# Splitting weights early and moving the decisions of a bitwise top-k search to GpSimd, in a two-layer encoder on one Trainium2 core

## The chip, the cores and the metric

The kernel runs on one core of one Trainium2 chip. The engines are named as in the profile: PE (TensorE matmul), PEld (its weight loads), DVE (VectorE), ACT (ScalarE), POOL (GpSimd) and SP (SyncE, which here only issues transfers). The metric is the device time of one execution in microseconds. PE's clock has two levels, 1.2 and 2.4 GHz; the profile gives the granted share of full speed.

## The reference

A trunk of two layers over 1040 tokens (16 meta tokens and 1024 frames) of width 1024. Layer 0 mixes tokens by chunked gated linear attention (GLA), layer 1 by sparse attention (DSA), and each is followed by a SwiGLU FFN. Of the DSA layer, this matters here:

```
proj = h @ w_in                              # split: q, c, q_idx, k_idx, w_idx
c = rmsnorm(c, g_kv)                         # latent, 256 wide
s_idx = einsum('bqhd,bsd->bqhs', qib, k_idx) * IDX_DIM ** -0.5
score = einsum('bqhs,bqh->bqs', relu(s_idx), wb)
score = where(key_chunk <= q_chunk, score, -inf)
top_val, top_idx = lax.top_k(score, 256)     # 256 keys per query
...
logits = q . (c[top_idx] @ w_uk) + bias[top_idx]
p = softmax(where(valid, logits, -inf)); o = (p @ c_sel) @ w_uv; return o @ w_out
swiglu(h) = (silu(h @ w_gate) * (h @ w_up)) @ w_out
```

All of it is float32. The selection by `top_k` is exact: ties go to the lower index.

## The kernel before

**Precision.** A float32 product is made of three matmuls in a faster format (`fp32r`): each operand is split into a high half (a cast) and a low half (operand minus high), and `PE` adds high x high, low x high and high x low (lines 198 to 200). So each weight tile that is loaded has to be split: `load_split` loads pieces of up to 1056 columns into a raw slot on SP's queue, ACT casts the high half (L186; GpSimd in the search, L188), and DVE or GpSimd subtracts for the low one (L189). Activations are split by `split` (L193 on ACT, L194 on DVE or GpSimd). Split weights stand in a ring of slots (`wh`, `wl`); `Weights.get` hands out a weight and loads the next one.

**Stages.** GLA to about 430 us; first FFN to 1245; index keys, index queries and scores to about 1382; the top-k search to about 1566 and the masks to 1605; attention to about 1850; then the attention's output weights and the second FFN. In the FFN a hidden unit (`hidden`) multiplies 128 gate and 128 up columns for a chunk of about 344 tokens, has ACT take silu into a slot `sg` of three, and has DVE multiply.

**The top-k search** (`topk`). Scores stand in `sc`, one block of 128 queries x nkeys, with nkeys 272, 400, 528, 656, 784, 912 and 1040 for blocks 1 to 7. For each query the 256th largest score is found bit by bit: a candidate threshold is counted against the keys, and the count decides the bit. The seven blocks form two groups, A (blocks 7, 1, 4, 3) and B (5, 2, 6). ACT counts 7 and 1 of A and 5 of B (L1047, a sign with an accumulator), DVE the others (L1053, a compare with an accumulator). Bits 31 to 16 are searched on the upper 16 bits of each score read as a bfloat16 number; bits 31 and 23 are counted on DVE alone. After each count come tiny operations on one column per block, all on DVE: `below` (L1062), `cand` (L1070), `flip` (L1073) and a second `flip` (L1076) in the upper half. `turnover` then takes the lower 16 bits of the keys that equal the threshold, as ordered numbers (ACT, L1103), and bits 15 to 0 follow with L1114, L1115 and L1117. While one group's tiny operations wait, the other group is counted: `rounds` writes them interleaved. At the end the seven masks are made (L1166 to L1174), with a running sum over ties.

**What runs beside it.** While the search goes, the code also emits PE's work in units: nine latent tiles (`latent`: 256 columns, root mean square by `row_rstd`, six tiny operations and a square root for each tile, then two transposes), 24 query units (`queries`, one head and a third of the frames each, drained by ACT into `qf`, L1000), the splits of queries (`parts`, L194; heads 3 to 5 on GpSimd) and the keys of the first head pair. Each unit has a cost, and as the units' costs add up, one step of the search is emitted for each share. Engines work their queues in the order of emission.

Of the kernel before, what the change touches and what calls it, by code (L numbers as in the profile page):

```python
# [22 lines left out]
TOPK = 256  # L23
# [56 lines left out]
class Weights:  # L80
# [28 lines left out]
class Trunk:  # L109
    def __init__(self, ctx, tc, io, out):  # L110
# [9 lines left out]
        self.whigh = None  # L120
# [55 lines left out]
    def load_split(self, src, n, pool=None, tags=("wh", "wl"), cap=RING, raw=None, piece=RAW):  # L176
# [4 lines left out]
        for a in range(0, n, piece):  # L181
            e = min(n, a + piece)
            r = raw() if raw else self.rawp.tile([128, RAW], F32, name="wraw")
            nc.sync.dma_start(r[:, : e - a], src[:, a:e])
            if self.whigh is None:
                nc.scalar.copy(hi[:, a:e], r[:, : e - a])  # L186
            else:
                self.whigh.tensor_copy(hi[:, a:e], r[:, : e - a])  # L188
# [474 lines left out]
    def ffn(self, pool, tmp, chunks, last_chunks, squares, after):  # L663
# [4 lines left out]
        def hidden(hh, hl, wi, q, a, n):  # L668
# [4 lines left out]
            t = tmp.tile([128, 512], F32, name="t")  # L673
# [21 lines left out]
        for g in range(G):  # L695
# [53 lines left out]
            prev = (hh, hl)  # L749

    def ffn_phase(self, layer, begun, norm_row, last_chunks, after, emit=None, cover=()):
# [3 lines left out]
        with ExitStack() as ctx:  # L755
# [36 lines left out]
            self.ffn(pool, tmp, chunks, last_chunks, squares, ended)  # L792
# [7 lines left out]
    def index_begin(self):  # L800
# [7 lines left out]
        def first():  # L808
            self.wlow = self.nc.gpsimd
# [11 lines left out]
    def dsa(self):  # L821
# [3 lines left out]
        with ExitStack() as ctx:  # L825
            self.wlow = nc.gpsimd
# [78 lines left out]
            with tc.tile_pool(name="topk", bufs=1) as tp, tc.tile_pool(name="cn", bufs=2) as cp:  # L905
# [3 lines left out]
                self.whigh = nc.gpsimd  # L909

                def parts(c, j):
# [3 lines left out]
                    self.split(self.xh[:, hs, t], self.xl[:, hs, t], qf[:, hs, a - META : a - META + n],  # L915
# [38 lines left out]
    def latent(self, pool, qf, cth, ctl):  # L954
# [5 lines left out]
        def unit(i):  # L960
            if i == 0:
                st["w"] = w.get("c")
# [514 lines left out]
```

## Time and profile before

| | |
|---|---|
| median of 3 runs | 2663.42 us (2662.87 to 2664.26) |
| profiled execution | 2667.23 us, its span 2665.0 us |
| mean granted clock of PE | 0.975 |
| PE busy | 2530.1 us, 95% of the span |
| DVE busy | 1417.1 us, 53% |
| ACT busy | 965.7 us, 36% |
| POOL busy | 255.2 us, 10% |
| weights in the DSA layer's queue | kidx, qidx (2), c, dq (4), ukv (4), do (4) |

The busy shares are averages over stages with different limits: 53% of DVE over the span says nothing of the 220 us in which it works without a break. The profiled execution is 3.8 us longer than the median, and sums over its rows are to be made against 2667.2. Times of day in the rows (1508.29) count from the span's start. Operations on one engine overlap by some hundredths of a microsecond, so that durations add up to slightly more than the busy time.

### The profile page before, as it was taken

What the parts mean: (1) busy time and instruction counts of PE and PEld (TensorE: products, weight loads), DVE (VectorE), ACT (ScalarE), POOL (GpSimd) and SP (SyncE); (2) the same over time, 40 slices, a digit from 0 to 9 for tenths busy, and PEclk for the clock granted to TensorE, in tenths of its full rate; (3) what the DMA queues carried; (4) which work ended last, traced back from release to release, by engine and by line L of the source; (5) the groups of instructions that cost most, each with busy time, mean ns of one, the idle gap of its engine ahead of it and who ended that gap; (6) DMA issues with size and microseconds to landing.
All of it is one profiled execution on the core that took longest, in us unless ns stands there. A gap on an engine that the chain in (4) does not pass through costs nothing.

```text
span 2665.0 us, 37404 instructions
## 1 busy us (share of the span) xinstructions
PE 2530.1 (95%) x15072; PEld 2342.3 (88%) x15072; DVE 1417.1 (53%) x3196; ACT 965.7 (36%) x1981; POOL 255.2 (10%) x222
## 2 busy tenths in 40 slices
PE   7999999999999999999898749999999999999997
PEld 6899999999999999999778739999988888888887
DVE  7565565643333333345699997673633333333346
ACT  5654452521111111114475667772511111111114
POOL 3000000200000000001212125540200000000001
PEclk9899999999999999999998969999999999999999
DMA  3113113011111111112100001012011111111111
GB/s 116 40 35 105 39 38 108 32 53 43 48 48 48 48 48 48 48 56 91 39 17 33 25 1 41 25 45 107 32 48 48 48 48 48 48 48 48 48 48 64
DMA packets 45168, 133.32 MB, mean 50 GB/s; under 512 B 4442, under 2 KB 15986, under 8 KB 44995
## 3 DMA queue, kind: packets, MB, share of 16 engines
q1 hardware_dynamic: 43634, 125.99, 14.0%
q0 software_dynamic: 1360, 4.95, 0.7%
q8 instruction: 118, 1.93, 0.3%
q14 instruction: 56, 0.45, 0.1%
HBM read 122.43 MB, written 13.27 MB: 51 GB/s over the span
## 4 chain that ended last, share of the span: by engine, by line
PE 79%; DVE 12%; issue 4%; ACT 3%; POOL 1%; DMA 0%; SPq 0%; ACTq 0%; DVEq 0%; POOLq 0%
PE ps L198 25%; PE ps L200 25%; PE ps L199 25%; DVE jd L1053 4%; PE ps L1282 1%; DVE sc L877 1%; POOL xl L194 1%; PE ps L499 1%; DVE no L304 1%; DVE xl L194 0%; DVE flip L1073 0%; PE ps L218 0%; PE ps L1294 0%; ACT L292 0%; DVE na L267 0%
## 5 line engine op out<-in xcount | busy, mean ns | idle before, releaser
L198 PE MATMUL ps<-xh,wh 128*128 128x344 f32 (+6 forms) x2808 | 951.0, 339 | 21.8 <-ACT qf L1000 12.3
L200 PE MATMUL ps<-xh,wl 128*128 128x344 f32 (+6 forms) x2808 | 944.2, 336 | 3.5 <-DVE wl L189 3.1
L199 PE MATMUL ps<-xl,wh 128*128 128x344 f32 (+6 forms) x2808 | 946.1, 337 | 1.3 <-POOL xl L194 0.9
L198 PEld LDWEIGHTS ps<-xh,wh 128*128 128x128 f32 x2808 | 532.2, 190 | 55.9 <-ACT qf L1000 14.7
L199 PEld LDWEIGHTS ps<-xl,wh 128*128 128x128 f32 x2808 | 532.5, 190 | 31.2 <-POOL xl L194 1.8
L200 PEld LDWEIGHTS ps<-xh,wl 128*128 128x128 f32 x2808 | 532.5, 190 | 30.6 <-DVE wl L189 3.3
L675 DVE TENSOR_TENSOR t<-sg,ps 128x344 f32<-128x344 f32 (+4 forms) x116 | 65.1, 561 | 653.5 <-PE ps L200 652.6
L186 ACT CAST wh<-wraw 128x1056 fp32r<-128x1056 f32 (+2 forms) x175 | 179.4, 1049 | 593.4 <-PE ps L199 588.3
L688 DVE TENSOR_TENSOR h<-h,ps 128x344 f32<-128x344 f32 (+3 forms) x456 | 251.3, 567 | 168.0 <-PE ps L200 167.9
L198 PE MATMUL ps<-hh,wh 128*128 128x512 f32 (+2 forms) x800 | 280.3, 350 | 0.0
L199 PE MATMUL ps<-hl,wh 128*128 128x512 f32 (+2 forms) x800 | 280.0, 350 | 0.0
L200 PE MATMUL ps<-hh,wl 128*128 128x512 f32 (+2 forms) x800 | 279.8, 350 | 0.0
L189 DVE TENSOR_TENSOR wl<-wraw,wh 128x1056 fp32r<-128x1056 f32 (+2 forms) x167 | 201.8, 1230 | 78.0 <-ACT wh L186 77.0
L198 PE MATMUL ps<-wh,xh 128*128 128x256 f32 (+9 forms) x560 | 174.8, 312 | 16.1 <-ACT xh L193 6.9
L200 PE MATMUL ps<-wh,xl 128*128 128x256 f32 (+9 forms) x560 | 168.7, 301 | 3.6 <-POOL xl L194 1.6
L194 POOL TENSOR_TENSOR xl<-no,xh 128x344 fp32r<-128x344 f32 (+5 forms) x52 | 59.5, 1150 | 1164.6 <-ACT xh L193 1164.5
L674 ACT ACTIVATE sg<-ps 128x344 f32<-128x344 f32 (+4 forms) x116 | 57.8, 498 | 304.0 <-PE ps L200 303.9
L199 PE MATMUL ps<-wl,xh 128*128 128x256 f32 (+9 forms) x560 | 167.2, 299 | 0.0
L193 ACT CAST hh<-t 128x344 fp32r<-128x344 f32 (+4 forms) x116 | 60.0, 517 | 285.0 <-DVE t L675 285.0
L198 PEld LDWEIGHTS ps<-hh,wh 128*128 128x128 f32 x800 | 150.0, 188 | 14.6
L199 PEld LDWEIGHTS ps<-hl,wh 128*128 128x128 f32 x800 | 150.3, 188 | 14.3
L200 PEld LDWEIGHTS ps<-hh,wl 128*128 128x128 f32 x800 | 150.5, 188 | 13.9
(283 smaller groups left out, 3376.4 us busy)
## 6 DMA issues: line engine op xcount, KB each, us to landing
wraw<-in_w_fi SPq DMA_DIRECT2D x44, 528.0 KB, 3.7
wraw<-in_w_fi SPq DMA_DIRECT2D x44, 496.0 KB, 4.8
wraw<-in_w_fo SPq DMA_DIRECT2D x22, 528.0 KB, 3.8
wraw<-in_w_fo SPq DMA_DIRECT2D x22, 496.0 KB, 4.8
s_skew<-s_rel POOLq DMA_DIRECT2D x8, 583.5 KB, 12.5
h<-in_ht SPq DMA_DIRECT2D x8, 520.0 KB, 5.5
wraw<-s_skew SPq DMA_DIRECT2D x8, 520.0 KB, 3.4
h<-s_h SPq DMA_DIRECT2D x8, 512.0 KB, 6.1
```

Of the source, the lines that this page charges most:

```text
L186: nc.scalar.copy(hi[:, a:e], r[:, : e - a])
L189: self.wlow.tensor_sub(lo[:, a:e], r[:, : e - a], hi[:, a:e].bitcast(F32))
L193: self.nc.scalar.copy(hi, src)
L194: (low or self.nc.vector).tensor_sub(lo, src, hi.bitcast(F32))
L198: mm(p, sh, mh, start=first, stop=False, skip_group_check=True)
L199: mm(p, sh, ml, start=False, stop=False, skip_group_check=True)
L200: mm(p, sl, mh, start=False, stop=last, skip_group_check=True)
L304: v.scalar_tensor_tensor(o, x, self.gains[:, row, k : k + 1], y, op0=OP.mult, op1=OP.mult)
L674: nc.scalar.activation(sg[:, :n], pg[:, :n], AF.Silu)
L675: v.tensor_mul(t[:, :n], sg[:, :n], pu[:, :n])
L688: v.tensor_add(self.h[:, d, a : a + n], self.h[:, d, a : a + n], p[:, :n])
L1053: v.tensor_scalar(j[:, : nkeys(b)], src(b), cand, None, op0=op, op1=OP.add, accum_out=out)
```

## The change

Four things change.

**Weights split early** (`split_early`, `load_parts`). All weights of the DSA layer (kidx, qidx, c, dq, ukv, do: 54 pieces of 512 columns) are loaded in the first FFN, one piece after each call of `hidden`; GpSimd makes both halves (L213, L214), and SP stores them to HBM (L216). Where the DSA layer needs a weight, GpSimd's queue loads both halves (L200), and nothing is split there any more. `sg` slots hold the raw pieces, and `t` shrinks to 352 columns in layer 0.

**The upper half on ordered numbers** (`signs`). Instead of bit 31 on bfloat16 numbers, the sign is counted on DVE from the upper 16 bits as integers; then ACT rewrites each block's upper halves as ordered unsigned numbers, scaled by plus or minus one (L1147). The other 15 upper bits are searched as the lower 16 are, the same seven blocks on the same engines in each bit, with float candidates.

**Decisions on GpSimd** (`decide`). The tiny operations after a count are four on GpSimd: a subtraction (L1102), a compare and multiply (L1103), an addition that gives the candidate (L1104), and the next `flip` (L1106). They are kept in order by `issue_after`.

**Latent norms by three** (`row_rstd` on three columns): the tiny operations run once for three tiles. In the masks, compare and subtraction become one operation, and the queries' low halves on GpSimd are three instructions per chunk instead of one.

DVE's queue in the lower half of the search, two rounds before, word for word; names end in the number of the buffer: group A's count is cnt_13074, its candidate cand_13079, group B's cnt_13097 and cand_13102.

```order
L1053 TENSOR_SCALAR jd,cnt_13097<-mask,cand_13102 128x400
L1053 TENSOR_SCALAR jd,cnt_13097<-mask,cand_13102 128x912
L1114 TENSOR_TENSOR below_13078<-cnt_13074,thr_13077 128x4
L1115 SCALAR_TENSOR_TENSOR cand_13079<-below_13078,flip_13080 128x4
L1117 TENSOR_SCALAR flip_13080<-cand_13079 128x4
L1053 TENSOR_SCALAR jd,cnt_13074<-mask,cand_13079 128x656
L1053 TENSOR_SCALAR jd,cnt_13074<-mask,cand_13079 128x528
L1114 TENSOR_TENSOR below_13101<-cnt_13097,thr_13100 128x3
L1115 SCALAR_TENSOR_TENSOR cand_13102<-below_13101,flip_13103 128x3
```

The same queue after, in the upper half, from a round without other work (group A's candidate is cand_13479, group B's cand_13498):

```order
L1093 TENSOR_SCALAR jd,cnt_13475<-mask,cand_13479 128x656
L1093 TENSOR_SCALAR jd,cnt_13475<-mask,cand_13479 128x528
L1093 TENSOR_SCALAR jd,cnt_13494<-mask,cand_13498 128x400
L1093 TENSOR_SCALAR jd,cnt_13494<-mask,cand_13498 128x912
L1093 TENSOR_SCALAR jd,cnt_13475<-mask,cand_13479 128x656
```

What moved: nothing but counts is left between counts; the tiny operations are gone from this queue.

GpSimd's queue in the search before: splits of weights, the first head pair's bias, and the low halves of the queries.

```order
L188 CAST wh<-wraw 128x1056
L188 CAST wh<-wraw 128x992
L189 TENSOR_TENSOR wl<-wraw,wh 128x1056
L189 TENSOR_TENSOR wl<-wraw,wh 128x992
L188 CAST uh<-wraw 128x1024
L189 TENSOR_TENSOR ul<-wraw,uh 128x1024
L1235 TENSOR_TENSOR sc<-wraw,mask 128x144
L194 TENSOR_TENSOR xl<-qf,xh 128x3x344 x2
```

The same queue after, from the upper half, with the loads of one weight's halves (s_dq) and their waits:

```order
L1104 TENSOR_TENSOR cand_13498<-below_13497,flip_13499 128x3 [waits Pool_49]
L1106 TENSOR_SCALAR flip_13499<-cand_13498 128x3 [waits Pool_49]
L200 DMA wl<-s_dq_l 128x2048 [waits DMASW5_49,PE_49]
L1102 TENSOR_TENSOR below_13478<-cnt_13475,thr_13477 128x4 [waits DVE_49,Activation_49]
L200 DMA wh<-s_dq_h 128x2048 [waits DMASW4_49,PE_49]
L1103 TENSOR_SCALAR below_13478<-below_13478 128x4 [waits Pool_49]
L1104 TENSOR_TENSOR cand_13479<-below_13478,flip_13480 128x4 [waits Pool_49]
L1106 TENSOR_SCALAR flip_13480<-cand_13479 128x4 [waits Pool_49]
```

What moved: eight tiny operations a bit stand here, each with a wait for the one before it, and two loads stand between decisions and wait for PE.

SP's queue in the first FFN before:

```order
L184 DMA wraw<-in_w_fi 128x1056
L184 DMA wraw<-in_w_fi 128x992
L184 DMA wraw<-in_w_fi 128x1056
L184 DMA wraw<-in_w_fi 128x992
L184 DMA wraw<-in_w_fo 128x1056
L184 DMA wraw<-in_w_fo 128x992
```

And after, where each piece is a load and two stores:

```order
L190 DMA wraw<-in_w_fi 128x992 [waits DMAHW7_49,DVE_49]
L190 DMA wraw<-in_w_fo 128x1056 [waits DMAHW6_49,DVE_49]
L190 DMA wraw<-in_w_fo 128x992 [waits DMAHW7_49,DMAHW1_49,DVE_49]
L212 DMA sg<-in_w_qidx 128x512 [waits DMAHW3_49,DMAHW2_49]
L216 DMA s_qidx_h<-eh 128x512 [waits Pool_49]
L216 DMA s_qidx_l<-el 128x512 [waits DMAHW4_49,Pool_49]
L212 DMA sg<-in_w_qidx 128x512 [waits DMAHW5_49,DVE_49]
L216 DMA s_qidx_h<-eh 128x512 [waits Pool_49]
L216 DMA s_qidx_l<-el 128x512 [waits Pool_49]
```

What moved: three pieces stand between two FFN weights, and their stores wait for GpSimd.

The diff, cut to its core:

```diff
+            name, src, n = self.seq[i]
+            self.tiles[i] = self.k.load_parts(name, n) if src is None else self.k.load_split(src, n)
...
+    def load_parts(self, name, n, pool=None, tags=("wh", "wl"), cap=RING):
+
+        pool = pool or self.ring
+        ts = [pool.tile([128, cap], F32R, name=t) for t in tags]
+        for t, src in zip(ts, self.parts[name]):
+            self.nc.gpsimd.dma_start(t[:, :n], src)
+        return tuple(ts)
+
+    def split_early(self, pool, raw):
+
+        nc = self.nc
+        for name, src, n in self.early:
+            for a in range(0, n, PRE):
+                e = min(n, a + PRE)
+                r = raw()[:, : e - a]
+                hi = pool.tile([128, PRE], F32R, name="eh")[:, : e - a]
+                lo = pool.tile([128, PRE], F32R, name="el")[:, : e - a]
+                nc.sync.dma_start(r, src[:, a:e])
+                nc.gpsimd.tensor_copy(hi, r)
+                nc.gpsimd.tensor_sub(lo, r, hi.bitcast(F32))
+                for p, t in zip(self.parts[name], (hi, lo)):
+                    nc.sync.dma_start(p[:, a:e], t.bitcast(F32))
+                yield
...
-        s = pool.tile([128, 4], F32, name="rs")
-        x, y, t, r = (s[:, j : j + 1] for j in range(4))
+        m = ss.shape[1]
+        s = pool.tile([128, 4 * m], F32, name="rs")
+        x, y, t, r = (s[:, j * m : j * m + m] for j in range(4))
...
                     wi = w.get("fi%d" % (2 * g + q))
                     for a, n in chunks:
                         hidden(hh, hl, wi, q, a, n)
+                        next(beside, None)
...
-                    self.split(self.xh[:, hs, t], self.xl[:, hs, t], qf[:, hs, a - META : a - META + n],
-                               nc.gpsimd if j in QPOOL else v)
+                    if j in QPOOL:
+                        for hd in range(3 * j, 3 * j + 3):
+                            self.split(self.xh[:, hd, t], self.xl[:, hd, t], qf[:, hd, a - META : a - META + n],
+                                       nc.gpsimd)
+                        return
...
+            y = self.row_rstd(pool, st["ss"], 256)
+            for i, c, x, r in st["x"]:
+                v.scalar_tensor_tensor(c[:r, :], x[:r, :], y[:r, i % 3 : i % 3 + 1], self.gkv[:r, :],
+                                       op0=OP.mult, op1=OP.mult)
+                self.later.at(3 + i % 3, lambda i=i, c=c: turn(i, c))
...
-        def upper(g, bit):
-            below, cand, flip, pos = (g[k] for k in ("below", "cand", "flip", "pos"))
-            steps = [lambda: v.tensor_tensor(below, g["cnt"], g["all" if bit in (31, 23) else "thr"],
-                                             op=OP.is_gt)]
-            if bit == 31:
-                steps += [lambda: v.tensor_scalar(cand, below, 31, 0x3FFFFFFF,
-                                                  op0=OP.logical_shift_left, op1=OP.bitwise_xor),
-                          lambda: v.tensor_scalar(pos, below, 1, None, op0=OP.bitwise_xor)]
-            else:
-
-                steps += [lambda: v.scalar_tensor_tensor(cand, below, bit, flip,
-                                                         op0=OP.logical_shift_left, op1=OP.bitwise_xor)]
-            if bit > 16:
-                steps += [lambda: v.scalar_tensor_tensor(flip, pos, bit - 1, cand,
-                                                         op0=OP.logical_shift_left, op1=OP.bitwise_xor)]
-            if bit > 17:
-                steps += [lambda: v.tensor_scalar(flip, flip, 1 << (bit - 2), None, op0=OP.bitwise_xor)]
-            return steps
+        def decide(g, bit):
+
+            below, cand, flip = g["below"], g["cand"], g["flip"]
+
+            with ExitStack() as after:
+                if last:
+                    after.enter_context(self.tc.issue_after(last[0]))
+                gp.tensor_sub(below, g["cnt"], g["thr"])
+                gp.tensor_scalar(below, below, 0.0, -(2.0 ** bit), op0=OP.is_gt, op1=OP.mult)
+                last[:] = [gp.tensor_add(cand, below, flip).ins]
+                if bit:
+                    last[:] = [gp.tensor_scalar_add(flip, cand, 2.0 ** (bit - 2) if bit > 1 else 0.5).ins]
+
+        def start(g, bits):
+            v.memset(g["cand"], 2.0 ** (bits - 1) - 0.5)
+            v.memset(g["flip"], 2.0 ** (bits - 1) + 2.0 ** (bits - 2) - 0.5)
...
+        def rounds(bits):
+            for bit in range(bits - 1, -1, -1):
+                for g in groups:
+                    if bit < bits - 1:
+                        decide(g, bit + 1)
+                    count(g)
+                    yield
...
+        def signs(g):
+            for c, b in enumerate(g["b"]):
+                n = nkeys(b)
+                j = pool.tile([128, T], BF16, name="jd", tag="pre", bufs=2)
+                v.tensor_scalar(j[:, :n], half(b, 1), 2.0 ** 15, None, op0=OP.is_ge, op1=OP.add,
+                                accum_out=g["cnt"][:, c : c + 1])
+            sgn, add, x, y = (g[k] for k in ("sgn", "add", "x", "y"))
+            v.tensor_tensor(x, g["cnt"], g["all"], op=OP.is_gt)
+            v.tensor_scalar(sgn, x, -2.0, 1.0, op0=OP.mult, op1=OP.add)
+            v.tensor_scalar(add, x, 65535.0, None, op0=OP.mult)
+            v.scalar_tensor_tensor(y, x, -1.0, g["cnt"], op0=OP.add, op1=OP.mult)
+            more(g, y)
+            start(g, 15)
+            for c in list(range(g["na"], g["n"])) + list(range(g["na"])):
+                b = g["b"][c]
+                nc.scalar.activation(mu(b), half(b, 1), AF.Identity, bias=add[:, c : c + 1],
+                                     scale=sgn[:, c : c + 1])
...
-            v.tensor_scalar(eq, pre, need, None, op0=OP.is_le)
-            v.tensor_sub(sg, sg, eq)
-            v.tensor_scalar(mk(b), sg, 0.0, NEG, op0=OP.is_ge, op1=OP.mult)
+            v.scalar_tensor_tensor(sg, pre, need, sg, op0=OP.is_le, op1=OP.subtract)
+            v.tensor_scalar(mk(b), sg, 0.0, NEG, op0=OP.is_le, op1=OP.mult)
```

## Rows read from the trace of the kernel before

**Rows 1.** Windows by stage: us, busy us of each engine (count), PEclk, DMA share, GB/s.

```profile
600.00:650.00 50.00, 50.00 (x318) 50.00 (x318) 14.86 (x25) 9.00 (x15) 0.00 (x0) 1.00 0.16 55
1280.00:1360.00 80.00, 72.49 (x351) 62.43 (x349) 54.77 (x101) 45.85 (x102) 21.71 (x13) 0.91 0.12 42
1386.00:1478.50 92.50, 78.87 (x509) 77.59 (x508) 91.36 (x323) 46.11 (x119) 24.05 (x15) 0.93 0.12 39
1478.50:1500.50 22.00, 18.41 (x96) 17.66 (x96) 21.12 (x70) 12.88 (x24) 0.00 (x0) 0.84 0.02 8
1500.50:1566.40 65.90, 32.30 (x156) 29.29 (x156) 63.96 (x206) 47.64 (x102) 4.73 (x2) 0.75 0.00 1
1566.40:1605.00 38.60, 23.18 (x102) 18.72 (x103) 38.24 (x111) 20.39 (x53) 14.41 (x9) 0.68 0.00 0
```

**Rows 2.** What PE waited for, 1380 to 1610: us, times, longest.

```profile
PE ps L198 <- DVE xl L1009: 26.3, 3, 13.6
```

**Rows 3.** Timeline of DVE, one bit of the lower half: start us, us, operation.

```profile
1508.29 0.62 DVE L1053 TENSOR_SCALAR_CACHE_REDUCE jd<-mask,cand 128x400 bf16<-128x400 uint16 x1
...
1508.84 1.16 DVE L1053 TENSOR_SCALAR_CACHE_REDUCE jd<-mask,cand 128x912 bf16<-128x912 uint16 x1
...
1509.92 0.16 DVE L1114 TENSOR_TENSOR below<-cnt,thr 128x4 f32<-128x4 f32 x1
...
1510.39 0.89 DVE L1053 TENSOR_SCALAR_CACHE_REDUCE jd<-mask,cand 128x656 bf16<-128x656 uint16 x1
...
1511.89 0.15 DVE L1114 TENSOR_TENSOR below<-cnt,thr 128x3 f32<-128x3 f32 x1
...
1512.36 0.62 DVE L1053 TENSOR_SCALAR_CACHE_REDUCE jd<-mask,cand 128x400 bf16<-128x400 uint16 x1
```

**Rows 4.** Instruction groups of DVE, 1375 to 1605: count, busy us, mean ns, idle before.

```profile
L1073 DVE SCALAR_TENSOR_TENSOR flip<-pos,cand 128x4 int32<-128x4 int32 (+1 forms) x30 | 12.1, 403 | 0.5
...
L1062 DVE TENSOR_TENSOR below<-cnt,thr 128x4 int32<-128x4 f32 (+1 forms) x28 | 9.1, 327 | 0.0
L1070 DVE SCALAR_TENSOR_TENSOR cand<-below,flip 128x4 int32<-128x4 int32 (+1 forms) x30 | 8.4, 279 | 0.5
...
L1076 DVE TENSOR_SCALAR flip<-flip 128x4 int32<-128x4 int32 (+1 forms) x28 | 5.6, 199 | 0.0
```

**Rows 5.** Timeline of all engines, 1441 to 1449.

```profile
1443.78 4.77 POOL L189 TENSOR_TENSOR wl<-wraw,wh 128x1056 fp32r<-128x1056 f32 x2
...
1443.87 2.40 DVE L1073 SCALAR_TENSOR_TENSOR flip<-pos,cand 128x4 int32<-128x4 int32 x1
```

**Rows 6.** Instruction groups of ACT's counts, 1375 to 1605.

```profile
L1047 ACT ACTIVATE ja<-mask,cand 128x1040 bf16<-128x1040 uint16 (+5 forms) x90 | 78.5, 872 | 58.0 <-DVE cand L1070 31.3 <-DVE cand L1115 22.2 <-DVE cand L1065 2.9
L1047 ACT ACTIVATION_READ_ACCUMULATOR ja<-mask,cand 128x1 f32 x90 | 16.9, 188 | 0.0
```

**Rows 7.** Instruction groups of POOL by shape, whole span.

```profile
L194 POOL TENSOR_TENSOR xl<-no,xh 128x344 fp32r<-128x344 f32 x24 | 30.3, 1270 | 137.4 <-ACT xh L193 137.4
...
L332 POOL TENSOR_SCALAR w<-mean 96x128 fp32r<-96x128 f32 x4 | 2.0, 534 | 0.0
...
L194 POOL TENSOR_TENSOR xl<-no,xh 128x144 fp32r<-128x144 f32 x4 | 2.9, 727 | 4.1 <-ACT xh L193 4.1
...
L972 POOL MEMSET css<- 128x1 f32 x1 | 0.2, 186 | 0.0
```

**Rows 8.** Instruction groups of DVE's score sums by shape, 1300 to 1390.

```profile
L877 DVE SCALAR_TENSOR_TENSOR sc<-rt,wx,sc 128x328 f32<-128x328 f32 x14 | 6.7, 554 | 0.0
...
L877 DVE SCALAR_TENSOR_TENSOR sc<-rt,wx,sc 128x272 f32<-128x272 f32 x7 | 6.2, 891 | 0.2
```

**Rows 9.** The page: a PE group, a DMA queue, an FFN weight's load.

```profile
L200 PE MATMUL ps<-xh,wl 128*128 128x344 f32 (+6 forms) x2808 | 944.2, 336 | 3.5 <-DVE wl L189 3.1
...
q0 software_dynamic: 1360, 4.95, 0.7%
...
wraw<-in_w_fo SPq DMA_DIRECT2D x22, 528.0 KB, 3.8
```

More of the change, by code (lines that the diff above doesn't have):

```diff
@@ L958, in latent @@
         st = {}
+        slot = lambda j: qf.rearrange("p h t -> p (h t)")[:, j * 256 : j * 256 + 256]
         def unit(i):
@@ L1040, in count @@
-        def count(g, op, all_v=False, src=mk):
-            vs = []
-            for c, b in enumerate(g["b"]):
-                cand, out = g["cand"][:, c : c + 1].bitcast(F32), g["cnt"][:, c : c + 1]
-                if c < g["na"] and not all_v:
+        groups, last = [], []
+        for j, (blocks, na) in enumerate(GROUPS):
+            g = {"b": blocks, "n": len(blocks), "na": na}
+            for name, dt in (("cnt", F32), ("all", F32), ("thr", F32), ("below", F32), ("cand", F32),
+                             ("flip", F32), ("sgn", F32), ("add", F32), ("th", I32), ("x", F32), ("y", F32)):
+                g[name] = pool.tile([128, g["n"]], dt, name=f"{name}{j}")
+            for c, b in enumerate(blocks):
+                v.memset(g["all"][:, c : c + 1], nkeys(b) - float(TOPK))
+                v.memset(g["thr"][:, c : c + 1], nkeys(b) - (2.0 if c < na else 1.0) * TOPK)
+            groups.append(g)
@@ L1109, in turnover @@
-            v.memset(cand.bitcast(F32), 2.0 ** 15 - 0.5)
-            v.memset(g["flip"].bitcast(F32), 2.0 ** 15 + 2.0 ** 14 - 0.5)
-        def lower(g, bit):
-            below, cand, flip = (g[k].bitcast(F32) for k in ("below", "cand", "flip"))
-            return [lambda: v.tensor_tensor(below, g["cnt"], g["thr"], op=OP.is_gt),
-                    lambda: v.scalar_tensor_tensor(cand, below, -(2.0 ** bit), flip, op0=OP.mult,
-                                                   op1=OP.add),
-                    lambda: v.tensor_scalar(flip, cand, 2.0 ** (bit - 2) if bit > 1 else 0.5, None,
-                                            op0=OP.add)]
@@ L1120, in rounds @@
-        def rounds(bits, decide, op, src=mk):
-            counts, carry = [], []
-            for bit in bits:
-                for g in groups:
-                    tiny = decide(g, bit + 1) if bit < bits[0] else []
-                    for x in tiny[:1] + carry + counts[:1] + tiny[1:2]:
-                        x()
-                    rest = counts[1:]
-                    counts = count(g, op(bit), bit in (31, 23), src)
-                    for x in rest + tiny[2:3]:
-                        x()
-                    carry = tiny[3:]
-                    yield
-            for x in carry + counts:
-                x()
@@ L1138, in topk @@
-        for b in range(1, 8):
-            (v.tensor_copy if b % 2 else nc.scalar.copy)(mk(b).bitcast(U16), half(b, 1))
-        yield
-        yield from rounds(range(31, 15, -1), upper, lambda bit: OP.is_lt if bit == 31 else OP.is_le)
-        for g in groups:
-            for x in upper(g, 16):
-                x()
+                low = pool.tile([128, T], U16, name="low", tag="sg", bufs=2)[:, :n]
+                nc.scalar.activation(low, half(b, 0), AF.Identity, bias=g["add"][:, c : c + 1],
+                                     scale=g["sgn"][:, c : c + 1])
@@ L1145, in topk @@
+                v.scalar_tensor_tensor(mu(b), mu(b), tc, low, op0=OP.is_equal, op1=OP.mult)
+            more(g, g["cnt"])
+            bits_of(g, 1)
+            start(g, 16)
+        for g in groups:
+            signs(g)
+            yield
+        yield from rounds(15)
+        for g in groups:
+            decide(g, 0)
             turnover(g)
             yield
-        yield from rounds(range(15, -1, -1), lower, lambda bit: OP.is_lt, lambda b: mk(b).bitcast(U16))
+        yield from rounds(16)
```

159 lines of the change are left out of this document (70 added, 89 removed).

## The prediction

> **What bounds the kernel now.** I read the windows by stage first, then what TensorE waits for, then single instructions of one stage. In the windows [rows 1] the reader is to look at the two busy columns of PE and DVE. In a slice of the first FFN PE is busy 50.00 of 50 us and DVE 14.86: that stage is PE's, and everything else there is beside it. Between 1386 and 1605, the search for the 256 best keys and the masks, it is the other way round: DVE is busy 91.36 of 92.5, 21.12 of 22.0, 63.96 of 65.9 and 38.24 of 38.6 us, PE only 78.87, 18.41, 32.30 and 23.18. So PE stands still for 66 of these 219 us. Its largest wait is for DVE: 26.3 us in three waits for the low halves of the last queries [rows 2], which DVE reaches only in its turn between counts. A change is worth there what it takes off DVE, until the next engine binds.
>
> One bit of the lower half (one row for each group of blocks) is read from the timeline [rows 3]: group B's counts run 1508.29 to 1509.92 (1.63 us), three tiny operations to 1510.39 (0.47), group A's counts to 1511.89 (1.50), three tiny ones to 1512.36 (0.47): 4.07 us, of which 3.13 are counting. In the upper half the same bit takes far longer: the four tiny groups there sum to 9.1 + 12.1 + 8.4 + 5.6 = 35.2 us [rows 4], because some are stretched. One flip, of a kind that lasts 0.16 us undisturbed [rows 3], lasts 2.40 us while GpSimd subtracts weights from 1443.78 on for 4.77 us [rows 5].
>
> **The change, part by part.** The sum is made against the profiled execution, 2667.2 us (span 2665.0 and 2.2 around it), 3.8 us above the median of 2663.4; the 3.8 is taken off at the end.
>
> *The length of a bit afterwards.* Four things can set it, and the longest does. DVE: 3.13, counts alone. ACT: its counts and accumulator reads are (78.5 + 16.9) / 30 = 3.18 us a bit [rows 6], a little less where spans overlap; it drains queries too, so about 3.4. GpSimd: eight tiny operations, four a group. No row has a tiny operation on it. The nearest are a memset of one column, 186 ns, and a tensor_scalar of 128 columns, 534 ns; two subtractions of 144 and 344 columns, 727 and 1270 ns, lie on a line that starts at 0.34 and rises by 2.7 ns a column [rows 7]. I take 0.35, the line's start, since four columns add 0.01; eight make 2.8 (1.5 to 4.3 by the ends). The loop of group A: ACT's part of its counts, 1312 of 2096 columns of 3.18, is 2.0; then three operations until the candidate stands, 1.05; two hand-overs between engines, for which no row stands and I put 0.1 each, an estimate below the 0.16 that a tiny operation on DVE takes with all its passing on (three dependent ones in 0.47); together 3.25. I take 3.4. The bounds are 3.13, where only counting is left, and 4.3, where an operation costs 0.534.
>
> *Upper half* (92.5 us). Counting took 14 bits at 3.13 and bit 23 with all seven on DVE, and the rest of bit 31: 43.8 + 6.0 + 4.1 = 54 (the three blocks that ACT has elsewhere, 2.9 us, from the slope of [rows 3]: 400 columns 0.62, 912 columns 1.16). The tiny operations overlap their neighbours by some 0.08 each (1508.29 + 0.62 is later than 1508.84), so 116 of them take 35.2 - 9 = 26. That leaves 11 for latents. Afterwards: 15 bits of counting, 47; latents 8, since 36 of 54 tiny operations of their norms go, at 0.08 to 0.2 each (3 taken of 3 to 7); sign counts 4 and their dozen tiny operations 2; three exposed while ACT turns seven blocks into ordered numbers, for 4592 columns at ACT's 3.18 / 2096 per column make 7 us, partly beside the other group's sign counts; and 15 times the 0.27 between 3.13 and 3.4, 4. Sum 68: **24.5 saved** (31 without the last two, 11 at 4.3).
>
> *Turnover* (22.0): the same seven counts, conversions and writes; the clamp and the sign arithmetic go, two candidates now come over GpSimd. **2** (0 to 4).
>
> *Lower half* (65.9): 16 × 3.4 = 54.4, and 1 us of other work as now (65.9 - 16 × 4.07). What is new in GpSimd's queue: the low halves of three heads stand there as three instructions of 344 columns in front of a decision, 3 × 1.27 = 3.8 us, twice within the search, of which some 2.5 is exposed each time, less 2 for what ran beside. 58: **8 saved** (15 at 3.13; 9 lost at 4.3 with both blocks exposed).
>
> *Masks* (38.6): seven pairs of wide operations become one each. An operation of 400 to 912 columns takes 0.62 to 1.16 as a count [rows 3]; seven at 0.6 are 4. **2** (0 to 4), as other work fills this stage too.
>
> *Index and scores* (1280 to 1360). GpSimd no longer splits weights beside DVE. Of the score sums that ran beside it, 272 columns took 891 ns, and 328 without it 554 [rows 8]. PE stands still for 80.00 - 72.49 = 7.5 us there [rows 1], which is the upper end, and 0 the lower; **4**, the middle, since PE also waits there for things that stay.
>
> *Attention and its output weights.* PE waits 3.1 us for DVE's weight splits over the whole run [rows 9], most of which go here; three key halves arrive split. **2** (0 to 5).
>
> *What is paid, at nothing.* In the first FFN 54 pieces are loaded, split on GpSimd and stored. A subtraction of 512 columns is 1.7 by the line of [rows 7], the cast no more, so under 2 × 1.7 × 54 = 184 us of GpSimd, which is busy 0.00 in this stage [rows 1]. Queue of SP: a piece's two stores wait for GpSimd, and the next FFN weights' loads stand behind them. A piece is a load of half of 528 KB, which lands in 3.8 [rows 9], and up to 3.4 of splitting, three of them at most 21.6 us; PE spends 50.00 / 318 = 0.157 us on a matmul [rows 1], 7.5 on a hidden unit of 48, 22.6 on the three of one weight, so the loads still come in time, if closely; if the cover failed by 1 us a piece it would cost 54. The slots of sg, now shared by pieces and gates, turn over every one and a half units, and a piece holds one for about 7 us. DVE, which GpSimd may block, has 35 of 50 us free. The loads of the split weights move to GpSimd's queue and wait there for TensorE to free the slot, with a decision behind. ACT's drain of a query waits for the same TensorE work, so this adds the issue alone. That queue moved 4.95 MB in 0.7% of the span [rows 9], 265 GB/s, by which a weight's 2 MB take 8 us, against the 22 us that PE spends on its six query units of 24 matmuls (78.87 / 509 = 0.155 each [rows 1]).
>
> Sum: 24.5 + 2 + 8 + 2 + 4 + 2 = 42.5. 2667.2 - 42.5 = 2624.7, less 3.8: **2621 us**.
>
> **The rivals.**
> *GpSimd's chain decides (slower).* What becomes of the bit when each tiny operation has to wait for the one before it through a semaphore: 0.534, plus 0.16 for the passing on, is 0.69; eight are 5.6 us a bit. 31 × (5.6 - 3.4) = 68 more, so 2621 + 68 = 2689. It decides from 42.5 / 31 = 1.4 above 3.4, at 4.8 us a bit or 0.60 an operation. For it: every tiny operation of GpSimd waits for the previous one in the order. Against: the line that starts at 0.34. [...]
> *GpSimd's queue binds a little.* At 0.534 without hand-overs a bit is 4.3: 31 × 0.9 = 28 more, 2649.
> *Everything hides.* 3.13 a bit, all upper ends: 31 + 4 + 15 + 4 + 7.5 + 5 = 66.5, 2597. For it: DVE alone is the bound now. Against: ACT's 3.18.
> *The first FFN pays.* 1 us a piece, 54: 2675. Against: PE at 50.00 of 50 with loads issued far ahead.
>
> **How the numbers follow.** Forecast 0.57, everything hides 0.17, a little bound 0.14, GpSimd's chain 0.09, FFN 0.03. About 0.2% (5 us) is what a measurement tells from no change. Faster therefore 0.86 (the first three, less 0.02), the same 0.02 (where the little bound grows), slower 0.12. The forecast's own range is 2610 to 2635; the range given runs from 2596, all hidden, to 2655, past the little bound.
>
> **What would show it.** The tiny rows vanish from DVE, and GpSimd has 62 decisions of four; the lower half's period, from one count of 400 columns to the next, is 3.2 to 3.6. DVE's count follows GpSimd's candidate at 0.1, an operation there lasts about 0.35 from start to start. The first FFN still shows PE at 50 of 50. The forecast is wrong if DVE stands idle over 1 us a bit for GpSimd, or if the score stage loses what the search gives.

## The result, and the profile after

The changed kernel takes 2605.93 us, the median of 4 runs (2604.56 to 2606.86), against 2663.74 for the kernel before: a ratio of 0.9783, 95% interval 0.9766 to 0.9800. That is 57.8 us less, where 42.5 were forecast; 2605.93 lies in the range given (2596 to 2655), 15 us under the predicted 2621. Its profiled execution has a span of 2604.0 us, 61.0 under the one of before (2665.0, an execution 3.8 us above its median).

The windows by stage, to be read against [rows 1] (us, then busy us of PE, PEld, DVE, ACT and POOL, each with its count, then PE's clock, DMA share, GB/s):

```profile
600.00:650.00 50.00, 50.00 (x319) 50.00 (x317) 15.71 (x26) 9.01 (x15) 11.59 (x12) 1.00 0.43 147
1280.00:1357.50 77.50, 73.26 (x354) 59.16 (x353) 50.78 (x107) 44.86 (x103) 6.91 (x10) 0.96 0.23 84
...
1381.10:1443.70 62.60, 55.16 (x371) 54.88 (x371) 58.05 (x167) 54.77 (x131) 29.10 (x123) 0.92 0.18 68
1443.70:1454.00 10.30, 10.30 (x68) 10.30 (x67) 10.13 (x30) 5.15 (x8) 0.61 (x1) 1.00 0.05 8
1454.00:1512.40 58.40, 50.06 (x312) 49.33 (x310) 56.62 (x139) 51.49 (x118) 34.64 (x127) 0.94 0.10 36
1512.40:1548.20 35.80, 20.76 (x83) 18.06 (x83) 34.74 (x89) 17.53 (x45) 13.24 (x18) 0.60 0.08 29
```

The first FFN is PE's as before, with GpSimd at work beside it. In the search DVE is still the busiest engine, but PE now follows closely: 115.5 of the 131.3 us up to the masks, with the clock at 0.92 to 1.00. In the masks DVE is full as before, and PE is busy 20.76 of 35.8 us at a granted clock of 0.60, between its two levels.

One bit of the lower half on DVE, as in [rows 3] (start, length, operation):

```profile
1463.70 0.62 DVE L1093 TENSOR_SCALAR_CACHE_REDUCE jd<-mask,cand 128x400 bf16<-128x400 uint16 x1
...
1464.25 1.16 DVE L1093 TENSOR_SCALAR_CACHE_REDUCE jd<-mask,cand 128x912 bf16<-128x912 uint16 x1
...
1465.33 0.89 DVE L1093 TENSOR_SCALAR_CACHE_REDUCE jd<-mask,cand 128x656 bf16<-128x656 uint16 x1
...
1466.15 0.76 DVE L1093 TENSOR_SCALAR_CACHE_REDUCE jd<-mask,cand 128x528 bf16<-128x528 uint16 x1
...
1466.83 0.62 DVE L1093 TENSOR_SCALAR_CACHE_REDUCE jd<-mask,cand 128x400 bf16<-128x400 uint16 x1
```

And GpSimd in the same bit:

```profile
1463.93 0.20 POOL L1102 TENSOR_TENSOR below<-cnt,thr 128x4 f32<-128x4 f32 x1 [0.34 <-DVE jd L1093]
1464.22 0.26 POOL L1103 TENSOR_SCALAR below<-below 128x4 f32<-128x4 f32 x1
1464.56 0.20 POOL L1104 TENSOR_TENSOR cand<-below,flip 128x4 f32<-128x4 f32 x1
1464.85 0.23 POOL L1106 TENSOR_SCALAR flip<-cand 128x4 f32<-128x4 f32 x1
1465.56 0.20 POOL L1102 TENSOR_TENSOR below<-cnt,thr 128x3 f32<-128x3 f32 x1 [0.49 <-DVE jd L1093]
```

The period is 1466.83 - 1463.70 = 3.13 us in place of 4.07: counting and nothing else. Group A's candidate ends at 1464.56 + 0.20 = 1464.76, and DVE is still counting group B until 1465.33. A decision takes 1.15 us (1463.93 to 1465.08), an operation 0.29 to 0.34 from start to start, and GpSimd stands idle before each decision.

The 61.0 us between the two spans, by marks that both traces have (a stage ends where its last instruction of the named kind ends or starts):

| stage, end mark | before | after | saved | forecast |
|---|---|---|---|---|
| all up to the last score sum | 1381.0 | 1374.5 | 6.5 | 4 |
| upper half, to the first rewritten block | 102.9 | 73.1 | 29.8 | 24.5 |
| turnover and lower half, to the last count | 82.5 | 64.9 | 17.6 | 10 |
| masks | 39.1 | 35.7 | 3.4 | 2 |
| attention to the end | 1059.5 | 1055.8 | 3.7 | 2 |

Run again, the changed kernel has the three rows of the search and the masks within 0.1 us. The first mark lies between 1373.3 and 1376.9 in ten executions of kernels that are alike up to it, so the first row is good to some 3 us only.

### The profile page after: what moved, and what is told of

Its sections match the earlier page's. It is cut to its first block, busy times and chain, and to the rows that moved or that the text cites. A ratio compares the mean times of both kernels' runs of the same rounds, so it can differ in the third digit from the quotient of the medians.

```text
span 2604.0 us, 37955 instructions
## 1 busy us (share of the span) xinstructions
PE 2513.8 (97%) x15072; PEld 2333.6 (90%) x15072; DVE 1358.0 (52%) x2915; ACT 952.7 (37%) x1970; POOL 382.0 (15%) x582
## 3 DMA queue, kind: packets, MB, share of 16 engines
q1 hardware_dynamic: 62642, 154.31, 17.6%
## 4 chain that ended last, share of the span: by engine, by line
PE 41%; DVE 4%; issue 2%; ACT 2%; POOL 1%; DMA 0%; ACTq 0%; DVEq 0%; POOLq 0%
PE ps L226 13%; PE ps L227 13%; PE ps L225 13%; PE ps L1310 1%; DVE jd L1093 1%; POOL xl L221 1%; DVE sc L912 1%; PE ps L1322 1%; PE ps L903 0%; DVE pre L1197 0%; ACT ja L1090 0%; ACT rt L907 0%; PE ps L1298 0%; PE ps L905 0%; DVE h L332 0%
## 5 line engine op out<-in xcount | busy, mean ns | idle before, releaser
L191 ACT CAST wh<-wraw 128x1056 fp32r<-128x1056 f32 (+2 forms) x160 | 163.9, 1049 | 582.4 <-PE ps L226 570.8
L192 DVE TENSOR_TENSOR wl<-wraw,wh 128x1056 fp32r<-128x1056 f32 (+2 forms) x158 | 195.1, 1257 | 73.8 <-ACT wh L191 72.9
L702 ACT ACTIVATE sg<-ps 128x344 f32<-128x344 f32 (+4 forms) x116 | 57.8, 498 | 303.5 <-PE ps L227 299.0
L225 PEld LDWEIGHTS ps<-wh,xh 128*128 128x128 f32 x560 | 109.6, 196 | 17.7 <-ACT xh L220 8.1
```

Of the source, the lines that this page charges most:

```text
L225: mm(p, sh, mh, start=first, stop=False, skip_group_check=True)
L702: nc.scalar.activation(sg[:, :n], pg[:, :n], AF.Silu)
```

## The experiments

All are compared with the kernel before on the same chip, as ratios; the changed kernel itself, run again beside three of them, gave 0.9775 (0.9761 to 0.9788, 2606.09 us).

| kernel | us | ratio to the kernel before, 95% |
|---|---|---|
| decisions on DVE | 2627.61 | 0.9858 (0.9844 to 0.9873) |
| weights split late | 2632.05 | 0.9873 (0.9858 to 0.9888) |
| only weights split early | 2636.76 | 0.9890 (0.9873 to 0.9906) |
| four more operations in a decision | 2643.13 | 0.9913 (0.9898 to 0.9928) |
| two more | 2615.33 | 0.9812 (0.9799 to 0.9826) |
| latents' norms one by one | 2606.97 | 0.9779 (0.9766 to 0.9792) |
| masks with two operations | 2606.14 | 0.9774 (0.9760 to 0.9787) |
| low halves spread | 2604.78 | 0.9771 (0.9757 to 0.9784) |
| spread, mask step 4.5 | 2608.28 | 0.9785 (0.9772 to 0.9799) |
| spread, mask step 7.0 | 2609.52 | 0.9790 (0.9776 to 0.9803) |

For the changed kernel beside them:

> The changed kernel again, for the small differences of the three kernels beside it: 2606 us, ratio to the kernel before 0.978.

**Decisions back on DVE.**

```diff
-                gp.tensor_sub(below, g["cnt"], g["thr"])
-                gp.tensor_scalar(below, below, 0.0, -(2.0 ** bit), op0=OP.is_gt, op1=OP.mult)
-                last[:] = [gp.tensor_add(cand, below, flip).ins]
+            v.tensor_tensor(below, g["cnt"], g["thr"], op=OP.is_gt)
+            v.scalar_tensor_tensor(cand, below, -(2.0 ** bit), flip, op0=OP.mult, op1=OP.add)
...
```

> The changed kernel with its decisions back on DVE, in three tiny operations a group. Theory D (a bit lasts as long as DVE's own work in it): the period of the lower half goes from 3.13 to 4.07 us, as in the kernel before (two times 0.47 more), 31 bits x 0.94 = 29 us: 2606 + 29 = 2635 us (2625 to 2645). Rival W (most of the gain comes from weights split early, which stretched DVE's tiny operations): undisturbed tiny operations hide between counts, at most 10 us: up to 2616. Rival P (GpSimd's chain binds the changed kernel): the same or faster.

2627.61 us, above what W allows and at the lower end of D: by the ratios 20 to 22 us are given back. The period of the lower half is what theory D says, 4.07 (1491.32 to 1495.39, timeline of DVE):

```profile
1491.32 0.62 DVE L1093 TENSOR_SCALAR_CACHE_REDUCE jd<-mask,cand 128x400 bf16<-128x400 uint16 x1
...
1492.95 0.16 DVE L1099 TENSOR_TENSOR below<-cnt,thr 128x4 f32<-128x4 f32 x1
...
1495.39 0.62 DVE L1093 TENSOR_SCALAR_CACHE_REDUCE jd<-mask,cand 128x400 bf16<-128x400 uint16 x1
```

Turnover and lower half take 77.1 us in place of 64.9, the upper half 81.9 in place of 73.1. So turnover and lower half pay most of the 0.94 a bit (12.2 of 15), the upper half only 8.8 of 14; there DVE waits 3.5 us for GpSimd's candidates in the changed kernel, and such waits are gone. P is refuted.

**Weights split late.** The search, latents and masks as changed, all weights split where they are used, as before.

```diff
-            self.tiles[i] = self.k.load_parts(name, n) if src is None else self.k.load_split(src, n)
+            self.tiles[i] = self.k.load_split(src, n)
...
+                self.whigh = nc.gpsimd
```

> The changed search, latents and masks, but the DSA layer's weights are split where they are used, as in the kernel before, in the search on GpSimd. Theory D: the score stage gives back its 6.5 us, and in the search three weights of 6.8 us and a key weight of 3.5 stand in GpSimd's queue in front of decisions, up to 24 us: 2606 + 6 to 30, 2628 as the middle. Rival W: nearly all of the 58 us are lost, over 2648. If GpSimd's splits lay beside the search without harm: 2612.

2632.05, near the middle of D. What happens is seen in GpSimd's queue (timeline): a decision of group B can start only when 6.8 us of splits are done, and DVE waits 5.68 us for its candidate (last line).

```profile
1442.90 0.23 POOL L1076 TENSOR_SCALAR flip<-cand 128x4 f32<-128x4 f32 x1
1443.08 2.03 POOL L189 CAST wh<-wraw 128x1056 fp32r<-128x1056 f32 x2
1445.07 4.76 POOL L190 TENSOR_TENSOR wl<-wraw,wh 128x1056 fp32r<-128x1056 f32 x2
1449.80 0.19 POOL L1072 TENSOR_TENSOR below<-cnt,thr 128x3 f32<-128x3 f32 x1
```

```profile
1450.66 0.63 DVE L1063 TENSOR_SCALAR_CACHE_REDUCE jd<-mask,cand 128x400 bf16<-128x400 uint16 x1 [5.68 <-POOL cand L1074]
```

By the marks of the table above, 15.4 of the 24.3 us between the two spans lie in the search (7.3 in the upper half, 8.1 behind it), and DVE's counts wait 16.8 us for candidates there, in place of 5.2. All up to the last score sum gives back 4.5, and the attention 4.8, which D had not priced. So with decisions on GpSimd the early split is also what keeps its queue free.

**Only weights split early.**

```diff
-        seq += [("kidx", io["w_kidx"], 1024)]
...
+        seq += [(name, None, n) for name, _, n in self.early[:8]]
...
```

> The kernel before with weights split early and nothing else. Theory D: 6.5 us in index and scores and the stretched part of DVE's tiny operations, 35.2 - 116 x 0.16 = 17 us, are gained, attention 3: 2664 - 24 = 2640 (2632 to 2650). Rival W: most of the gain, 2606 to 2625. If the early splits cost as much in the first FFN as they save: 2660 or more.

2636.76, inside D's range, 29.4 under its chip's 2666.16. The groups of DVE's tiny operations, against [rows 4] (count, busy us, mean ns):

```profile
L1105 DVE SCALAR_TENSOR_TENSOR flip<-pos,cand 128x4 int32<-128x4 int32 (+1 forms) x30 | 5.0, 167 | 0.5
L1102 DVE SCALAR_TENSOR_TENSOR cand<-below,flip 128x4 int32<-128x4 int32 (+1 forms) x30 | 4.8, 159 | 0.5
L1108 DVE TENSOR_SCALAR flip<-flip 128x4 int32<-128x4 int32 (+1 forms) x28 | 4.5, 162 | 0.0
L1094 DVE TENSOR_TENSOR below<-cnt,thr 128x4 int32<-128x4 f32 (+1 forms) x28 | 4.3, 154 | 0.0
```

They sum to 18.6 us in place of 35.2, and the upper half is 86.3 us in place of 102.9: 16.6 in both. That is the stretch of [rows 5]; the rest of the upper half comes to the same length. The Trainium skill's SBUF — State Buffer, section "Who interferes with whom", on the port pair that DVE and GpSimd share, says that a DVE operation with two SBUF inputs contends with a GpSimd instruction that reads SBUF, that the pair is locked for one of them at a time, and that the form that writes out its accumulator cannot enter the modes that take it. The trace agrees: the flip, with two inputs, takes 403 ns on average before and 167 here, and counts of 912 columns, which write out an accumulator, take the same in the kernel before in its lower half (first line) and in its upper half, where GpSimd splits (second line).

```profile
L1053 DVE TENSOR_SCALAR_CACHE_REDUCE jd<-mask,cand 128x912 bf16<-128x912 uint16 x16 | 18.5, 1158 | 0.0
L1053 DVE TENSOR_SCALAR_CACHE_REDUCE jd<-mask,cand 128x912 bf16<-128x912 bf16 x16 | 18.5, 1154 | 0.0
```

The other 13 us come from all up to the last score sum (6.1) and the attention (7.0).

Between this kernel and the one with decisions on DVE, run on the same chip, lie 9.2 us: ordered numbers in the upper half (three tiny operations in place of four, bit 23 shared with ACT), latents and masks together.

**Four, then two more operations in each decision.**

```diff
                 gp.tensor_scalar(below, below, 0.0, -(2.0 ** bit), op0=OP.is_gt, op1=OP.mult)
+                for _ in range(4):
+                    gp.tensor_scalar(below, below, 0.0, 1.0, op0=OP.add, op1=OP.mult)
```

> The changed kernel with four more tiny operations in each decision on GpSimd (they leave the value as it is). If GpSimd's queue counts, 16 operations of 0.315 us are 5.05 us a bit in place of 3.13: 31 x 1.9 = 59 more, 2665, the time of the kernel before. If only the loop count-decision-count does: 2.85 + 4 x 0.33 = 4.2, 33 more, 2639. If GpSimd had room for it all: 2606.

2643.13: 35 to 37 us more by the ratios, near the 33 of the loop, but by another way. In the lower half GpSimd has no pause (timeline):

```profile
1522.62 0.20 POOL L1102 TENSOR_TENSOR below<-cnt,thr 128x4 f32<-128x4 f32 x1
...
1523.24 1.02 POOL L1105 TENSOR_SCALAR below<-below 128x4 f32<-128x4 f32 x4
...
1524.94 0.19 POOL L1102 TENSOR_TENSOR below<-cnt,thr 128x3 f32<-128x3 f32 x1
```

A decision of eight is 2.32 us, a bit 4.66 (1519.92 to 1524.58 on DVE): the queue binds, at 0.29 an operation and not the 0.315 I had put. Over all it costs less than 31 times 1.53: turnover and lower half pay 22.6 of 24.5 us, the upper half only 13.4 of 23. That DVE's latents fill a part of it there is likely, but was not tried.

The same with `range(2)`:

> The changed kernel with two more tiny operations in each decision (value unchanged). GpSimd's queue would then hold 12 operations a bit; at the 0.29 that the kernel with four more showed (16 in 4.66 us), 3.5 us a bit against DVE's 3.13: 0.37 more where DVE has nothing else, that is mainly in the lower half: 16 x 0.37 = 6 us, and up to 11 if the upper half pays too: 2612 to 2617. If only the loop counted: 2.85 + 2 x 0.29 = 3.43, 5 us in the lower half. If there were room: 2606.

2615.33, in the range, 8 to 10 us more by the ratios. A bit is 3.37 (1484.76 to 1488.13, DVE's counts of 656 columns), twelve operations at 0.28. By that, ten would take 2.8 to 2.9, so one more in each decision would about fit; it was not tried.

**Latents' norms one by one.**

```diff
-            y = self.row_rstd(pool, st["ss"], 256)
-            for i, c, x, r in st["x"]:
...
+            y = self.row_rstd(pool, ss, 256)
...
```

> The changed kernel with the latents' norms tile by tile, as in the kernel before (54 tiny operations on DVE in place of 18). Theory D: they stand on DVE in the upper half, which is busy 58.05 of 62.6 us there: 36 x 0.08 to 0.2 = 3 to 7 us more, about 2610. Rival (hidden: the upper half with latents is held by TensorE, 55 of 62.6 us, or by hand-overs): within 1 us.

2606.97 beside 2606.09: no difference that the time of the whole can show. The stage shows one: the upper half takes 74.9 us, and 73.1 in both executions of the changed kernel. So the term of 3 us is 1.8. Windows of the first 19 us of the counting, norms by three (the changed kernel run again) and one by one:

```profile
1381.00:1400.00 19.00, 11.54 (x79) 11.34 (x78) 15.95 (x56) 17.50 (x40) 6.06 (x26) 0.73 0.00 0
```

```profile
1381.00:1400.00 19.00, 12.14 (x100) 11.59 (x99) 17.65 (x74) 14.90 (x41) 5.87 (x25) 1.00 0.00 1
```

DVE is busy 1.7 us more in a stretch in which it otherwise waits. PE does 100 matmuls there in place of 79, at a granted clock of 1.00 in place of 0.73: by three, the first transposes wait 7.5 us at a stretch for the scaled tile, one by one 6.9 in three waits, the longest 3.0.

**Masks with two operations.**

```diff
-            v.scalar_tensor_tensor(sg, pre, need, sg, op0=OP.is_le, op1=OP.subtract)
+            v.tensor_scalar(eq, pre, need, None, op0=OP.is_le)
+            v.tensor_sub(sg, sg, eq)
...
```

> The changed kernel with the masks' compare and subtraction as two operations again. The prediction's term: 2 us (0 to 4) slower. What the new trace says: the one operation takes 1290 ns for 1040 columns where the two took 480 and 691, and 1156 for 912 where they took 443 and 619, so nothing was saved: the same, or faster by up to 1 us.

2606.14: the same, and the masks' stage too (35.8 us and 35.7). The fused operation of the changed kernel (first group below) takes a little longer than the two of the kernel before together (the other fence, 480 + 691 ns):

```profile
L1200 DVE SCALAR_TENSOR_TENSOR sg<-pre,y,sg 128x1040 bf16<-128x1040 f16 x1 | 1.3, 1290 | 0.0
```

```profile
L1172 DVE TENSOR_TENSOR sg<-sg,mask 128x1040 bf16<-128x1040 bf16 x1 | 0.7, 691 | 0.0
...
L1171 DVE TENSOR_SCALAR mask<-pre,y 128x1040 bf16<-128x1040 f16 x1 | 0.5, 480 | 0.0
```

**Low halves spread, and the pace of PE's units.** An attempt at a faster version.

```diff
-QPOOL, KEYS0, PC = (1,), 0, 1.0
+QPOOL, KEYS0, PC = (3, 4, 5), 0, 0.5
...
-                    units += [(PC, lambda c=c, j=j: parts(c, j)) for j in range(2)]
+                    units += [(PC, lambda c=c: parts(c, 0))]
+                    units += [(PC, lambda c=c, j=j: parts(c, j)) for j in (3, 4, 5)]
```

> The changed kernel with the queries' three low halves on GpSimd emitted as three units of their own, so that decisions can stand between them. In the changed trace DVE waits 1.61 us and ACT 3.02 behind one block of three (3.71 us), and the last decision of the search waits some 2.5 us behind another. If such a block costs what DVE waits: 3 to 5 us faster, 2602. Rival (TensorE or the masks give it back): within 1 us.

2604.78: 1.3 us below the changed kernel in the medians and inside both intervals, so not shown to be faster; in the one trace the lower half and the masks are 0.4 us shorter each. In the changed kernel such a block stands in front of a decision for 3.71 us, and DVE waits 1.61 of them (timeline of POOL, then of DVE):

```profile
1495.87 3.71 POOL L221 TENSOR_TENSOR xl<-qf,xh 128x344 fp32r<-128x344 f32 x3
1499.53 0.20 POOL L1102 TENSOR_TENSOR below<-cnt,thr 128x4 f32<-128x4 f32 x1
```

```profile
1500.40 0.90 DVE L1093 TENSOR_SCALAR_CACHE_REDUCE jd<-mask,cand 128x656 bf16<-128x656 uint16 x1 [1.61 <-POOL cand L1104]
```

Spread, the first block parts around a decision, but the second still stands in one piece ahead of the last decision (3.63 us at 1508.59), since no step of the search was emitted between its units.

With the cost of a mask step raised as well, so that PE's units are paced otherwise:

```diff
-MASK, D1, D2 = 2.5, 1, 2
+MASK, D1, D2 = 4.5, 1, 2
```

> The kernel with GpSimd's low halves spread, and the cost of a mask step set from 2.5 to 4.5, so that TensorE's units are spread over the search and the masks by the time that these now take. TensorE is busy 43.0 of 43 us in the upper half from 1400 on and 20.8 of 35.8 in the masks' stage. If the upper half waits for TensorE: 3 to 6 us faster than the changed kernel, 2600 to 2603. If DVE sets the end whatever TensorE does: within 2 us.

2608.28, no gain. The upper half got only 1.0 us shorter (72.1 in place of 73.1), though PE had less to do in it, 41.15 of the 43 us from 1400 on in place of 43.0 (windows of this kernel):

```profile
1400.00:1443.00 43.00, 41.15 (x282) 40.92 (x281) 41.42 (x115) 35.31 (x91) 22.00 (x93) 1.00 0.27 99
1443.00:1512.00 69.00, 61.14 (x389) 60.56 (x388) 68.45 (x177) 56.36 (x124) 33.87 (x135) 0.99 0.10 32
1512.00:1548.00 36.00, 18.22 (x86) 16.67 (x87) 35.84 (x72) 18.84 (x46) 17.18 (x14) 0.60 0.09 29
```

The last count ends at 1508.1 in place of 1512.5, and the masks end at 1553.8 in place of 1548.2. So DVE's work was moved, not shortened: from the last score sum to the end of the masks the stages take 178.3 us in place of 173.7, with DVE busy 35.84 of 36 us in the masks and PE 18.22.

And with 7.0:

> The same with a mask step at 7.0, so that still more of TensorE's units come late. If the upper half waits for TensorE: the search shorter again, but units then come after the masks; 2600 to 2606. If DVE sets the end: within 2 us of the changed kernel, or later by what TensorE has left after the masks.

2609.52: last count 1506.1, masks 1552.2, upper half 72.6. Both fit DVE setting the end of these stages; another pace of PE's units gave the upper half 1 us at most.

## Why the prediction was right, and where it was off

*DVE bounds the search, and a bit falls to what is left on it.* Shown: 3.13 after, 4.07 with the decisions back on DVE, 3.37 and 4.66 where GpSimd's queue is made longer. In the whole search of the changed kernel DVE's counts wait 5.2 us for GpSimd's candidates, in four waits: 0.17 us a bit, where over 1 was to be the sign that the forecast is wrong.

*Which terms missed.* The five rows of the table save 61.0 us where 42.5 were put, 18.5 more (15 in the medians, as the profiled execution before is 3.8 us above its median). The parts:

*The length of a bit, 3.4.* This term was mis-sized; it is 3.13. It rested on ACT's 3.18 a bit, spans and accumulator reads added up [rows 6]. They overlap, as ACT's timeline of the changed kernel shows in one bit:

```profile
1439.27 1.15 ACT L1090 ACTIVATE ja<-mask,cand 128x1040 bf16<-128x1040 uint16 x1
...
1440.41 0.51 ACT L1090 ACTIVATE ja<-mask,cand 128x272 bf16<-128x272 uint16 x1
...
1440.92 0.94 ACT L1090 ACTIVATE ja<-mask,cand 128x784 bf16<-128x784 uint16 x1
...
1441.85 0.43 ACT L1043 ACTIVATE qf<-ps 128x336 f32<-128x336 f32 x1
```

From 1439.27 to 1441.85 the three counts and their reads take 2.6 us, and a query's drain 0.43 follows: together 3.0. ACT was not the bound. In the lower half 0.27 too much is 4.3 us over 16 bits; the upper half's surplus has another source, below. "Everything hides" was right on this step (3.13 a bit); not all of its other upper ends were reached, hence 2606 and not 2597.

*GpSimd's operation, 0.35.* It is 0.29 to 0.34 from start to start for the dependent ones, 0.28 to 0.29 on average in a full queue; the line through wide operations [rows 7] gave its start well, the two nearest rows (0.186 and 0.534) did not. The rival that GpSimd's chain decides fails on this number: it asked for 0.60. A hand-over, put at 0.1, is 0.04 from GpSimd to DVE where DVE waits: the candidate ends at 1500.36, the count starts at 1500.40. The rule of the Trainium skill's GPSIMD Engine Reference, section 3.1, that DVE is the engine for elementwise work, holds for the single operation, 0.16 on DVE against 0.20 to 0.26 here, and a decision, 0.47 there, is 1.15 here; still the kernel with decisions on DVE is 20 to 22 us slower, since that work stood on the engine that sets the time.

*Upper half, 24.5.* It saved 29.8, and what was off is its length before. From the last score sum (1374.5) to the last count (1442.7) the changed kernel takes 68.2 us, and the prediction put 68. But the 92.5 us of before were taken from 1386.0 on, while the search begins at 1381.0, right behind the last score sum. In these 5 us DVE and ACT are nearly full, among other things with copies of the scores' upper halves (L1139) that the changed kernel does not make (window, busy us of PE, PEld, DVE, ACT; then DVE's timeline):

```profile
1381.00:1386.00 5.00, 5.00 (x45) 5.00 (x44) 4.42 (x38) 4.75 (x12) 0.00 (x0) 1.00 0.01 3
```

```profile
1382.47 1.51 DVE L1139 COPY mask<-sc 128x528 uint16<-128x528 uint16 x3
```

That the 68 came out is partly luck, as two of its terms cancel: DVE waits 3.9 us there (3.5 for GpSimd's candidates, 0.4 for ACT's rewriting) where 3 and 4 were put, and the latents' operations on DVE come to 10.4 us where 8 were. Of the 26 us of tiny operations before, 16.6 were the stretch, which goes with the weights alone; the prediction took both away at once and did not separate them. Its 3 for the norms were 1.8.

*Turnover and lower half, 2 and 8.* They saved 17.6. The bit gives 4.3 more than put. The turnover itself (first to last rewritten block) fell from 13.3 to 8.5, 4.8 where 2 were put. And the two blocks of low halves cost DVE less than the 2.5 us each that were put: 1.6 for the first, and 0.8 for the second, which falls into the masks.

*Masks, 2, and attention, 2.* The table has 3.4 and 3.7, but the two belong together. Masks and attention to the end take 1098.6 us before, 1091.5 with early weights alone and 1091.5 in the changed kernel. So the 7.1 come with the weights, and the 3.4 of the masks bring nothing to the end: attention's first score operations on DVE, which the kernel before does within its mask stage, mostly come after it in the changed kernel (windows of L1250 before, of L1278 after: us, then DVE's busy us):

```profile
1566.40:1605.50 39.10, 4.36 (x18) 0.68 0.00 0
```

```profile
1512.50:1548.20 35.70, 1.30 (x7) 0.60 0.08 29
```

The fused operation saved nothing, as its undoing shows. In the attention PE sets the time, and it is nearer to full in its first 250 us behind the masks, before and after:

```profile
1605.50:1855.50 250.00, 244.96 (x1846) 239.61 (x1846) 160.06 (x447) 157.57 (x389) 104.79 (x93) 1.00 0.15 54
```

```profile
1548.20:1798.20 250.00, 249.22 (x1884) 246.98 (x1885) 156.89 (x455) 152.26 (x382) 105.23 (x102) 0.99 0.20 72
```

The reason given for attention was wrong: PE's wait of 3.1 us for DVE's low halves [rows 9] is still there at 3.0. It belongs to an FFN weight that is split as before.

*Index and scores, 4.* Right: from the start of the first score sum to the end of the last it is 68.3 us before (1312.72 to 1381.00) and with late weights, and 64.1 after (1310.33 to 1374.46) and with early weights alone. The sums of 272 columns now take 501 ns in place of 891 [rows 8]. The rest of the row's 6.5 lies ahead of the scores, within what that mark varies from one execution to the next.

*The first FFN at nothing.* Right. From 520 to 1230 us (windows, before and then after):

```profile
520.00:1230.00 710.00, 710.00 (x4487) 709.88 (x4485) 267.82 (x454) 126.76 (x204) 4.26 (x4) 1.00 0.15 49
```

```profile
520.00:1230.00 710.00, 710.00 (x4486) 709.79 (x4485) 276.99 (x453) 126.75 (x204) 111.48 (x112) 1.00 0.33 109
```

PE has no pause in either; DVE pays 9.2 us beside GpSimd and has room for them.

The parts don't add up one by one. Early weights alone give 29.4; the rest alone, with late weights, some 34; both 57.8. The decisions on GpSimd are worth 20 to 22 with early weights and are hurt by late ones.

## What to carry to other kernels

Where one engine sets the time of a stage, move its small serial work to an idle engine even if that engine takes over twice as long for it, as long as another group's work covers the loop; then keep long operations out of that engine's queue. Measure an engine's share by the distance between starts, not by adding up spans, which overlap. And before a fused operation is counted as one pass, look whether the two that it replaces ran at a higher rate. And read what a stage saves together with the stage behind it: the 3.4 us that left the masks came back in the attention, where another engine sets the time.

## What the runs showed of the hardware that was not expected

A compare-and-subtract fused over f16 and bf16 columns takes 1290 ns for 1040 columns, while the compare alone takes 480 and the subtraction alone 691. On GpSimd four equal tiny operations in a row took 1.02 us, 0.26 each. And the loads of split weights on GpSimd's queue, 1024 KB each, landed 5.0 to 7.8 us after their issue (medians by load), with 0.53 to 0.61 us of GpSimd for the issue itself. On ACT the read of an accumulator, 0.19 us, did not add to the distance of the counts: counts of 1040, 272 and 784 columns, 1.15, 0.51 and 0.94 us long, started 1.14, 0.51 and 0.93 us before what came next.
